# A decoder layer on one core: where the second norm's scale and shift are applied, which engines do the last norm, and how many expert rows are gathered in the first half of the u stage

## The chip, the cores and the metric

One core of one Trainium2 chip runs the whole kernel. The metric is the device time of one execution in microseconds (us). "TensorE" and PE are the same engine, as are VectorE and DVE, ScalarE and ACT, GpSimd and POOL, SyncE and SP; the profile uses the short names. Line numbers (L1053) are those of the kernel before.

## The reference, cut to what matters

One layer, 256 tokens of width 2048, everything in float32. Two attention groups, then a product-key lookup of experts, then a gated embedding, each followed by a layer norm:

```python
x = layer_norm(alpha * x + mix_out, ln_g[0], ln_b[0])
# peer_ffn: 8 heads, top 16 of 128 x 128 keys each, so 128 experts for a token
act = gelu(einsum('thed,td->the', u[eidx], x)); ffn = einsum('the,thed->td', gates * act, v[eidx])
x = layer_norm(alpha * x + ffn, ln_g[1], ln_b[1])          # the second norm
gate = sigmoid(x @ ple_gate)                               # 2048 x 2048
x = layer_norm(alpha * x + gate * (p @ ple_proj), ln_g[2], ln_b[2])   # the last norm
# layer_norm(x, g, b) = (x - mean) * rsqrt(var + eps) * g + b over the 2048 columns
```

## The kernel before

**Stages in order.** The projections and the two attentions (0 to about 350 us), the output product and the first norm, the queries and their scores (to about 530 us), then the lookup, the second norm, the gate product and the last norm. Token tiles are 128 tokens; there are two (t = 0, 1). Natural rows are tokens by partition and columns along it; transposed tiles are columns by partition.

**The lookup.** For 156 of the 256 tokens the kernel computes all 16,384 experts: the u stage has 128 blocks `ia` of 128 experts each (`u_block`, L983: load 1 MB of `peer_u`, 16 matmuls in the source, each run as two on the chip), then the v stage runs over the same blocks twice, for the two halves of the output columns (`v_block`, L1064, half a MB for each block). The other 100 tokens (`NSP`) go another way: their chosen experts' rows are gathered, 100 gathers of `u_rows` and 100 of `v_rows`, each an indirect DMA of 128 rows of 8 KB (1 MB), and VectorE multiplies and sums them (L841, L851). `sparse_work` (L808) is a generator that issues one gather for each step. `gathers(n)` (L800) adds n to a running sum and takes a step for each whole one, so the constants set gathers per block: `GQ` 1.8 for a query, `GU` 0.64 for a block of u's first half (64 blocks, L1027), `GUG` 0.75 for its second, `GVG` 0.42 and `GV` 0.35 for the blocks of v. All that is left is issued near the end of v (three blocks before the six that are held back).

A gather waits for its place: ahead of each, SP moves one element to `mark` (L871) behind the weight loads that it has queued, and GpSimd copies it (L872) before it issues the gather (L874). There are four gather buffers (`NGB`); a buffer comes free when VectorE has used it. The top-16 selection (`topk_work`, L762) runs on VectorE as a generator too, one step for each block of u's first half, and its instructions and the uses of the gathers keep their program order on VectorE. Weights (`wf`, L105) are prefetched into five buffers by SP's queue.

**Order of instructions.** The framework orders the instructions of each engine by its own timeline estimate. `keep(...)` (`tc.keep_in_program_order`) pins an instruction: pinned instructions of an engine stay in the order of the source among themselves; others may move around them.

**End of v and residual rows.** The last six blocks are held back (`STAG`) and run for j = 0 to 7 (L1158), each j one column tile of 128. Between them stand `natural_out` (L891, the gathered tokens' sums), `third_sums`, and `res2` (L1105), which transposes finished column tiles of XF back into natural rows x2[t] and takes their statistics. `stats2` (L1190) holds mean, rstd and -mean*rstd for each token tile; the power is on GpSimd (L483).

**Second norm** (`ln2`, L1200). x2[t] is normed in four chunks of 512 columns, alternately on VectorE (L1208) and ScalarE (L1206), without g and b. TensorE transposes 16 tiles of 128 x 128 for each t (L1214), four to a PSUM bank. `ln_cols` (L501) applies g and b to each transposed tile, as a scale and a shift of each partition, alternately on VectorE (L510) and ScalarE (L507), into `ln_xx`; then ScalarE rounds two tiles at a time to the matmul's format as the high part (L518) and VectorE subtracts it for the low part (L519), both into X2. `LB` is the number of tiles at a time. The natural rows get g and b separately: `natural_x2` (L1262) loads them for one chunk, spread over all partitions, and GpSimd multiplies and adds (L1269, L1270).

**Gate product.** Four chunks c of 512 output columns. For each of 16 tiles k, each token tile takes three matmuls (`mm3`, L219: high by high, high by low, low by high). The weights of a chunk are 16 parts; `Stage.split` makes the high part on ScalarE (L115) and the low part on VectorE (L116); `sg2` holds eight parts, `sg` the other eight. `gate_out` (L1226) takes the sigmoid (L1234), multiplies with the embedding (L1235), adds (L1236) and takes statistics (L1239). In the last chunk token tile 1 is cut into two halves of 256 columns.

**Last norm** (`finish`, L1242), after both token tiles: columns up to 1600 (t = 0) or 1728 (t = 1) in two passes of VectorE, L1247 ((x - mean) * g) and L1255 (* rstd + b); the rest on ScalarE and GpSimd (L1250 to L1252). Each piece is stored by a DMA of its own.

## Time and profile before

| | us |
|---|---|
| median of 3 runs (lowest, highest) | 1787.52 (1786.72, 1788.03) |
| the profiled execution | 1785.93 |
| its span | 1784.2 |
| u's first half (64 blocks of 128) | about 532 to 808 |
| v, both column halves | about 1100 to 1671 |
| first gate matmul, last gate matmul ends | 1678.95, 1772.0 |

The profile is that of one execution. Its parts: busy time of the engines; the chain of waits (what released the instruction that ended last, followed back); groups of instructions by line with their mean duration; the timeline of one engine (start, duration, engine, line, operation, output <- input, count, and in brackets how long the engine had been idle and what released it); busy time in stretches. "PEld" is TensorE's weight load, which overlaps its matmuls. Times in timelines are us from the start of the span. A matmul's duration is longer than the distance to the next one, because matmuls are pipelined.

### The profile page before, as it was taken

How to read it: one execution, taken by the hardware profiler on the slowest of the kernel's cores; microseconds unless marked ns; L12 is line 12 of the kernel's file. 1: busy time of each engine (PE TensorE's matmuls, PEld its weight loads, DVE VectorE, ACT ScalarE, POOL GpSimd, SP SyncE). 2: the span in 40 equal slices, each digit the busy share in tenths (PEclk: the TensorE clock that was granted, in tenths of full speed). 3: DMA queues.
4: the chain of work that ended last, by engine and by line, in shares of the span. 5: the costliest groups of instructions: out<-in, count | busy, mean ns of one | idle time of the engine just before them, and what ended most of it. 6: DMA issues, size and time to landing. Idle time of an engine off the chain costs nothing.

```text
span 1784.2 us, 30408 instructions
## 1 busy us (share of the span) xinstructions
PE 1755.0 (98%) x12074; PEld 1646.9 (92%) x12074; DVE 1064.5 (60%) x1706; ACT 546.5 (31%) x1363; POOL 530.9 (30%) x576
## 2 busy tenths in 40 slices
PE   8999999999999999999999999999999999999997
PEld 6888888888889999999999999999999999999786
DVE  5555589654698868455555544966433334333777
ACT  5677478733110100103333313652000000000552
POOL 0133033105346227232233332323233323220232
PEclk9999999999999999999999999999999999999999
DMA  7544644567998999999999999999999999998481
GB/s 283 191 165 166 235 143 154 195 239 253 381 418 311 421 416 416 421 421 419 420 419 410 418 419 413 404 418 399 421 421 420 421 421 420 416 411 341 167 298 65
DMA packets 99695, 606.23 MB, mean 340 GB/s; under 512 B 12824, under 2 KB 14672, under 8 KB 35648
## 3 DMA queue, kind: packets, MB, share of 16 engines
q1 hardware_dynamic: 67792, 387.91, 55.0%
q0 software_dynamic: 30320, 213.62, 29.3%
q10 hardware_dynamic: 1440, 2.75, 0.4%
q8 instruction: 95, 1.56, 0.4%
q14 instruction: 48, 0.39, 0.1%
HBM read 598.36 MB, written 6.03 MB: 339 GB/s over the span
## 4 chain that ended last, share of the span: by engine, by line
PE 89%; DMA 8%; DVE 2%; ACT 1%; issue 0%; SPq 0%; DVEq 0%; ACTq 0%
PE ps_v L1053 30%; PE ps_u L215 26%; PE ps_qk L203 7%; PE ps_q L215 6%; DMA wf<-peer_u 5%; PE ps_qk L205 3%; PE ps_v L223 2%; PE ps_v L224 2%; PE ps_v L222 2%; PE ps_gate L223 1%; PE ps_gate L222 1%; PE ps_gate L224 1%; PE ps_mix L223 1%; PE ps_mix L224 1%; PE ps_mix L222 1%; DMA wf<-peer_v 1%
## 5 line engine op out<-in xcount | busy, mean ns | idle before, releaser
L1053 PE MATMUL ps_v<-A,wf 128*128 128x156 f32 x4096 | 551.9, 297 | 0.8 <-DMA wf<-peer_v 0.8
L1053 PEld LDWEIGHTS ps_v<-A,wf 128*128 128x128 f32 x4096 | 544.5, 190 | 1.8 <-DMA wf<-peer_v 1.3
L215 PE MATMUL ps_u<-XF,wf 128*128 128x156 f32 x3904 | 531.5, 297 | 5.9 <-DMA wf<-peer_u 4.5
L215 PEld LDWEIGHTS ps_u<-XF,wf 128*128 128x128 f32 x3904 | 519.6, 190 | 10.0 <-ACT A L986 5.6
L851 DVE SCALAR_TENSOR_TENSOR y<-gb,ew,y 128x2048 f32<-128x2048 f32 x94 | 220.8, 2349 | 222.0 <-DMA gb<-v_rows,eig 221.8
L841 DVE SCALAR_TENSOR_TENSOR gb<-gb,xq 128x2048 f32<-128x2048 f32 x100 | 231.5, 2319 | 147.7 <-DMA gb<-u_rows,eig 147.7
L116 DVE TENSOR_TENSOR wl<-wf,wh 128x1024 fp32r<-128x1024 f32 (+1 forms) x199 | 213.3, 1095 | 99.0 <-ACT wh L115 97.2
L872 POOL COPY pace<-mark 1x1 f32<-1x1 f32 x200 | 116.4, 582 | 513.9 <-DMA mark<-c_iota 513.4
L115 ACT CAST wh<-wf 128x1024 fp32r<-128x1024 f32 (+1 forms) x199 | 171.8, 893 | 151.3 <-PE ps_yn L897 39.8
L203 PE MATMUL ps_qk<-X,wh 128*128 128x512 f32 x512 | 185.2, 401 | 0.0
L986 ACT ACTIVATE A<-ps_u 128x156 f32<-128x156 f32 x128 | 38.4, 300 | 442.9 <-PE ps_u L215 357.0
L874 POOL DMA_INDIRECT gb<-u_rows,eig x100 | 114.7, 1147 | 143.7 <-DVE gb L841 74.7
L874 POOL DMA_INDIRECT gb<-v_rows,eig x100 | 123.4, 1234 | 78.4 <-DVE y L851 39.0
L205 PE MATMUL ps_qk<-X,wl 128*128 128x256 f32 x512 | 145.7, 285 | 0.0
L939 ACT ACTIVATE hi<-eq,ghf 128x64 f16<-128x64 f16 x312 | 104.5, 335 | 40.6 <-DVE eq L933 35.9
L203 PEld LDWEIGHTS ps_qk<-X,wh 128*128 128x128 f32 x512 | 96.4, 188 | 21.9 <-issue 1.0
L215 PE MATMUL ps_q<-XF,wf 128*128 128x256 f32 x512 | 113.6, 379 | 0.6 <-DVE XF L510 0.6
L1114 ACT COPY x<-ps_y 128x256 f32<-128x256 f32 (+3 forms) x12 | 5.2, 439 | 350.0 <-DVE st L1113 349.8
L215 PEld LDWEIGHTS ps_q<-XF,wf 128*128 128x128 f32 x512 | 95.9, 190 | 13.1 <-DVE XF L510 0.8
L940 ACT ACTIVATE lo<-eq,glf 128x64 f16<-128x64 f16 x312 | 104.1, 334 | 0.0
L205 PEld LDWEIGHTS ps_qk<-X,wl 128*128 128x128 f32 x512 | 96.3, 188 | 2.5 <-issue 1.3
L957 DVE SCALAR_TENSOR_TENSOR A<-ps_G,A 128x30 f32<-128x30 f32 (+2 forms) x96 | 32.6, 368 | 38.0 <-PE ps_G L947 21.9
(261 smaller groups left out, 1836.1 us busy)
## 6 DMA issues: line engine op xcount, KB each, us to landing
wf<-peer_v SPq DMA_DIRECT2D x128, 1024.0 KB
wf<-peer_u SPq DMA_DIRECT2D x122, 1024.0 KB
wf<-w_qk SPq DMA_DIRECT2D x64, 512.0 KB
wf<-w_out SPq DMA_DIRECT2D x32, 512.0 KB
wf<-peer_wq SPq DMA_DIRECT2D x16, 1024.0 KB
wf<-ple_gate SPq DMA_DIRECT2D x16, 1024.0 KB
wf<-w_v SPq DMA_DIRECT2D x31, 512.0 KB
early<-peer_u SPq DMA_DIRECT2D x6, 1024.0 KB
```

What stands on the lines that cost most here:

```text
L115: self.order(nc.scalar.copy(wh, src))
L116: self.order(nc.vector.tensor_tensor(wl, src, wh.bitcast(F32), op=ALU.subtract))
L203: nc.tensor.matmul(ps, wh[:, j * P:(j + 1) * P], xt[:, dt, :], start=dt == 0, stop=False)
L205: nc.tensor.matmul(ps[:, :T], wl[:, j * P:(j + 1) * P], xt[:, dt, :T], start=False, stop=dt == ND - 1)
L215: nc.tensor.matmul(ps[:, :T - t0], wf[:, dt * P:(dt + 1) * P], xt[:, dt, t0:], start=dt == 0, stop=dt == ND - 1)
L841: keep(nc.vector.scalar_tensor_tensor(g, g, 1.0, xq[i], op0=ALU.mult, op1=ALU.mult, accum_out=eact[i][:, j:j + 1]))
L851: keep(nc.vector.scalar_tensor_tensor(ys[i], g, ew[i][:, j:j + 1], ys[i], op0=ALU.mult, op1=ALU.add))
L872: keep(nc.gpsimd.tensor_copy(pace, mark))
L874: keep(nc.gpsimd.indirect_dma_start(out=g, out_offset=None, in_=a[kind], in_offset=bass.IndirectOffsetOnAxis(ap=eig[i][:, 0, j:j + 1], axi ...
L939: nc.scalar.mul(hi[:, j, :], eq[:, j, :], ghf[:, t])
L940: nc.scalar.mul(lo[:, j, :], eq[:, j, :], glf[:, t])
L1053: return nc.tensor.matmul(ps[:, (j % 2) * NDT:(j % 2 + 1) * NDT], vf[:, j * P:(j + 1) * P], W_of(ia), start=False, stop=ia == NIA - 1 and ...
```

## The change

It has four parts.

1. `GU` goes from 0.64 to 0.60. `GUG`, `GVG` and `GV` stay.
2. The second norm's g and b rows are loaded earlier, by SP, one chunk at a time into XF as its column tiles come free (`rows2`, pinned). For five of the eight pieces (token tile by chunk) VectorE applies norm, g and b to the natural rows in two passes ahead of the transposes: (x - mean) * g, then * rstd + b. For the other three (chunk 1 of t = 0, chunks 2 and 3 of t = 1) ScalarE norms them, applies g and b to the transposed tiles, and VectorE multiplies and adds g and b on the natural rows later. GpSimd does none of it.
3. For those five pieces the high and low parts come straight from the PSUM bank of the transposes, up to four tiles at a time (`ln2_hi`, `ln2_lo`). Everything from there to the end of the first gate chunk is pinned in an order written out by hand: transposes, parts, splits of the weights and gate matmuls of single k. The gate matmuls of the last chunk are pinned too, and in chunk 2 all splits for chunk 3 come ahead of token tile 1's `gate_out`.
4. The last norm is on VectorE alone. Token tile 0's statistics and first pass stand ahead of token tile 1's first half, its second pass ahead of the second half; the pieces are of 512 columns for t = 0 and 640, 640, 512, 256 for t = 1.

```diff
-GU, GUG = 0.64, 0.75
+GU, GUG = 0.60, 0.75
-LB = 2
+    gb2 = [XF[:, 4 * c:4 * c + 4, :].rearrange("p (i d) n -> p i (d n)", i=2) for c in range(NCH)]
+    def rows2(c):
+        for i, src in enumerate(("ln_g", "ln_b")):
+            keep(nc.sync.dma_start(
+                gb2[c][:, i], a[src][1:2, c * 512:(c + 1) * 512].to_broadcast([P, 512])))
...
         elif j == 6:
+            rows2(0)
...
         elif j == 7:
+            rows2(1)
...
+    rows2(2)
     res2(0, 12, 2)
...
+    def ln2_pass(i, t, c0, n):
+        mv, rstd, nmr = stats2[t]
+        s = slice(c0, c0 + n)
+        row = gb2[c0 // 512][:, i, c0 % 512:c0 % 512 + n]
+        if i == 0:
+            keep(nc.vector.scalar_tensor_tensor(x2[t][:, s], x2[t][:, s], mv[:, 0:1], row,
+                                                op0=ALU.subtract, op1=ALU.mult))
+        else:
+            keep(nc.vector.scalar_tensor_tensor(x2[t][:, s], x2[t][:, s], rstd, row,
+                                                op0=ALU.mult, op1=ALU.add))
+    def ln2_T(t, d0, nd):
+        ps = pbank(pp, "ps_x2T")
+        for j in range(nd):
+            keep(nc.tensor.transpose(ps[:, j * P:(j + 1) * P],
+                                     x2[t][:, (d0 + j) * P:(d0 + j + 1) * P], ident))
+        return ps[:, :nd * P].rearrange("p (j n) -> p j n", j=nd)
+    def ln2_hi(t, d0, src):
+        nd = src.shape[1]
+        keep(nc.scalar.copy(X2[:, d0:d0 + nd, t * P:(t + 1) * P], src))
+    def ln2_lo(t, d0, src):
+        nd = src.shape[1]
+        hi = X2[:, d0:d0 + nd, t * P:(t + 1) * P]
+        keep(nc.vector.tensor_tensor(X2[:, d0:d0 + nd, T + t * P:T + (t + 1) * P], src,
+                                     hi.bitcast(F32), op=ALU.subtract))
+    def act_norm(t, c):
...
+    def act_cols(d0, ps):
...
+    def natural_gb(t, c):
...
-    ln2(0)
-    ln2(1, range(ND // 8))
+    gw = [sg.load(a["ple_gate"][0, i]) for i in range(2, 4)]
+    rows2(3)
+    pss = [pbank(pa, "ps_gate") for _ in range(NT)]
+    act_norm(0, 1)
+    for i in range(2):
+        ln2_pass(i, 0, 0, 256)
+    ps = ln2_T(0, 0, 2)
+    ln2_hi(0, 0, ps)
+    ps1 = ln2_T(0, 4, 4)
+    for i in range(2):
+        ln2_pass(i, 0, 256, 256)
+    ps2 = ln2_T(0, 2, 2)
+    ln2_hi(0, 2, ps2)
+    ln2_lo(0, 0, ps)
+    gate_k(0, 0, 1)
+    ln2_lo(0, 2, ps2)
+    gate_k(0, 1, 3)
+    xx = act_cols(4, ps1)
+    ln2_hi(0, 4, xx)
+    ln2_pass(0, 1, 0, 512)
+    ln2_lo(0, 4, xx)
+    ln2_pass(1, 1, 0, 512)
+    both(1, 1)
+    gate_k(0, 3, 5)
+    ps = ln2_T(1, 0, 4)
+    ln2_hi(1, 0, ps)
+    gate_k(0, 5, 6)
+    ln2_lo(1, 0, ps)
+    act_norm(1, 2)
+    act_norm(1, 3)
+    more_parts(2)
+    gate_k(0, 6, 8)
+    gate_k(1, 0, 1)
+    ps = ln2_T(1, 4, 4)
+    ln2_hi(1, 4, ps)
+    ln2_lo(1, 4, ps)
+    gate_k(1, 1, 2)
+    both(0, 2)
...
+    gate_k(1, 6, 8)
+    gate_k(0, 8, 10)
+    ps = ln2_T(0, 12, 4)
+    ln2_hi(0, 12, ps)
+    ln2_lo(0, 12, ps)
+    more_parts(2)
+    gate_k(0, 10, 12)
+    for d0, k0, k1 in ((8, 12, 14), (12, 14, 16)):
+        ps = ln2_T(1, d0, 4)
+        xx = act_cols(d0, ps)
+        natural_gb(1, d0 // 4)
+        ln2_hi(1, d0, xx)
+        ln2_lo(1, d0, xx)
+        gate_k(0, k0, k1)
+    natural_gb(0, 1)
+    parts1 = list(sg2.parts(a["ple_gate"][1, 0]))
+    gate_k(1, 8, 16)
     for c in range(NCH):
         if c == NCH - 1:
+            pass2(0, [512, 1024, 1536], *mr)
             gate_out(c, 1, ps_half, 256, 256)
             break
...
-        natural_x2(c + 1, nc.sync)
...
+        gate_mm(pss[0], 0, parts, 0, 512, keep)
+        gate_mm(pss[1][:, :256], 1, parts, 0, 256, keep)
+        gate_mm(pss[2][:, :256], 1, parts, 256, 256, keep)
         gate_out(c + 1, 0, pss[0], 0, 512)
+        mr = finish_stats(0)
+        pass1(0, [512, 1024, 1536], *mr)
         gate_out(c + 1, 1, pss[1][:, :256], 0, 256)
         ps_half = pss[2][:, :256]
-    for t in range(NT):
-        finish(t, gr3, br3)
+    mr = finish_stats(1)
+    pass1(1, [640, 1280, 1792], *mr)
+    pass2(1, [640, 1280, 1792], *mr)
```

`act_norm(t, c)` norms 512 columns in place on ScalarE; `act_cols` applies g and b to four transposed tiles from PSUM, one activate for each; `natural_gb` is a multiplication and an addition of 512 columns on VectorE. `gate_k(t, k0, k1)` is `mm3` for single k, pinned; `both(t, c)` is the two passes over 512 columns; `more_parts(n)` splits n parts of the second half of chunk 0's weights; `finish_stats`, `pass1` and `pass2` are the parts of the former `finish`, without its share for ScalarE and GpSimd.

More of the change, by code (lines that the diff above doesn't have):

```diff
@@ new lines, in act_norm @@
+    def act_norm(t, c):
+        s = slice(c * 512, (c + 1) * 512)
+        mv, rstd, nmr = stats2[t]
+        keep(nc.scalar.activation(x2[t][:, s], x2[t][:, s], AF.Identity, bias=nmr, scale=rstd))
+    def act_cols(d0, ps):
+        xx = l2.tile([P, 4, P], F32, name="ln_xx", tag="ln_xx", bufs=2)
+        for j in range(4):
+            keep(nc.scalar.activation(xx[:, j], ps[:, j], AF.Identity,
+                                      bias=bT[:, 1, d0 + j:d0 + j + 1],
+                                      scale=gT[:, 1, d0 + j:d0 + j + 1]))
+        return xx
@@ L1273, in build, with finish_stats @@
-    sg.order = sg2.order = keep
-    parts = [parts0, gate_parts(0, 1)]
-    ln2(1, range(ND // 8, ND // 4))
+            keep(nc.vector.bn_stats(st3[t][:, 2 * c + j // 256, :],
+                                    x2[t][:, c * 512 + j:c * 512 + j + 256]))
+    def finish_stats(t):
+        mv = l2.tile([P, 2], F32, name="mv3", tag="ln_mv", bufs=2)
+        keep(nc.vector.bn_aggr(mv, st3[t]))
+        rstd = l2.tile([P, 1], F32, name="rstd3", tag="ln_rstd", bufs=2)
+        keep(nc.vector.tensor_scalar_add(rstd, mv[:, 1:2], LN_EPS))
+        nc.gpsimd.tensor_tensor(rstd, rstd, half_neg, op=ALU.pow)
+        return mv, rstd
@@ L1276, in build @@
+    ps = ln2_T(1, 0, 4)
[12 more added lines that the diff above has]
+    both(0, 2)
+    more_parts(1)
     for t in range(NT):
         keep(nc.scalar.copy(em3[:, t], pse[t]))
[L1278 to L1283 removed]
+    gate_k(1, 2, 6)
```

110 lines of the change are left out of this document (41 added, 69 removed).

## The prediction

> **What bounds the kernel now.** I read the page's engine table first, then busy time by stretches, then the timelines of the two places that the diff touches.
>
> ```profile
> PE 1755.0 (98%) x12074; PEld 1646.9 (92%) x12074; DVE 1064.5 (60%) x1706; ACT 546.5 (31%) x1363; POOL 530.9 (30%) x576
> 721.00:815.00 94.00, 89.99 (x668) 87.54 (x668) 45.45 (x51) 15.80 (x53) 28.84 (x31) 1.00 1.01 421
> 1240.00:1400.00 160.00, 160.00 (x1209) 160.00 (x1209) 65.87 (x31) 0.00 (x0) 50.40 (x55) 1.00 1.01 418
> 1600.00:1672.00 72.00, 72.00 (x538) 70.41 (x537) 31.46 (x48) 10.90 (x22) 3.50 (x4) 1.00 0.76 290
> 1672.00:1785.00 113.00, 96.29 (x475) 78.99 (x473) 87.31 (x152) 54.83 (x113) 36.28 (x32) 0.96 0.49 181
> ```
>
> A row of the stretches reads: stretch, its length, busy us and instructions of PE, PE's weight loads, DVE, ACT and POOL, TensorE clock, DMA share, GB/s. TensorE sets the time: it is idle only in u's first half (4.0 us in the second row) and in the last stretch (16.7 us). The clock is full. DMA moves 418 to 421 GB/s for as long as gathers run, so 1 MB (1,048,576 bytes) costs 2.49 us; after 1600 us it has room (share 0.76). So an edit is worth what it takes from those two idle places; elsewhere it must only not break TensorE's stream.
>
> **The change, part 1: fewer gathers in u's first half (GU 0.64 to 0.60).** TensorE's own timeline there:
>
> ```profile
> 648.54 72.33 PE ps_u L215 x544
> 734.19 4.48 PE L215 MATMUL ps_u<-XF,wf 128*128 128x156 f32 x32 [0.47 <-ACT A L986]
> 739.16 4.48 PE L215 MATMUL ps_u<-XF,wf 128*128 128x156 f32 x32 [0.49 <-DMA wf<-peer_u]
> ...
> 768.96 30.25 PE L215 MATMUL ps_u<-XF,wf 128*128 128x156 f32 x224 [0.48 <-ACT A L986]
> 799.70 4.48 PE L215 MATMUL ps_u<-XF,wf 128*128 128x156 f32 x32 [0.49 <-DMA wf<-peer_u]
> ```
>
> The first row (the chain of waits) gives a block of 32 matmuls undisturbed: 72.33 x 32 / 544 = 4.25 us. From 734.19 to 768.96 seven blocks take 34.77 us instead of 29.8: about 4.6 us lost once the three pairs of gate transposes between them are taken off, each block waiting for its `wf`. The stall at 799.70 adds 0.7. Why there? The gathers:
>
> ```profile
> 700.00:720.00 20.00, 5.28 (x6) 1.00 1.02 423
> 720.00:740.00 20.00, 3.83 (x4) 1.00 1.01 419
> 741.11 0.18 POOL L872 COPY pace<-mark 1x1 f32<-1x1 f32 x1 [1.37 <-DMA mark<-c_iota]
> ```
>
> (The first two rows are L874 alone: gathers issued per 20 us.) While DVE selects the top keys, gathers fall behind; then they catch up, 10 in the 40 us from 700. In those 40 us TensorE wants 40 / 4.25 = 9.4 MB of `peer_u` and the gathers bring 10 MB: 19.4 x 2.49 = 48.3 us of DMA in 40. The prefetched buffers cover some, TensorE waits for the rest. At 741 POOL waits for a mark again: the backlog is gone.
>
> With 0.60, 64 x 0.04 = 2.56 fewer gathers fall into this half. About 1.6 of them (40 blocks) lie ahead of the burst: 1.6 x 2.49 = 4.0 us of DMA time less, against 5.3 us lost. The steady need falls from 1.64 MB per 4.25 us (4.08 us of DMA, 96%) to 1.60 (3.98, 94%), so the stall at 799 should go too. Bounds: nothing (the burst is set by DVE's order, not by the marks) and 5.3. I take **4.0**, nearest to the DMA time that is removed.
>
> The 2.56 gathers land at the end of v's second half. Each needs 1 / 0.35 = 2.9 blocks of 2.1 us there, so the last gather comes about 15 us later than this row:
>
> ```profile
> 1613.77 0.96 POOL L874 DMA_INDIRECT gb<-v_rows,eig x1 [0.16 <-DVE gb L849]
> 1651.61 0.68 DVE L900 TENSOR_TENSOR x<-x,ps_yn 96x512 f32<-96x512 f32 x1 [24.36 <-PE ps_yn L897]
> ```
>
> The sums that need them start at 1651; the splits ahead of them (L115, L116 on `y`) move from 1607 to about 1622, the last use from 1625 to about 1640. That is the cover; its price if it were gone would be one us for each us past 1650. DMA has 0.24 x 72 = 17 us free there against 6.4 added. Cost: nothing.
>
> **Part 2: second norm and the start of the gate product.**
>
> ```profile
> 1672.33 2.74 PE L1124 MATMUL ps_emb<-wp,pf 128*128 128x512 f32 x6
> 1675.22 2.03 PE L1214 MATMUL ps_x2T<-ident,x 128*128 128x128 f32 x16 [0.15 <-DVE x L1208]
> 1678.95 0.50 PE L222 MATMUL ps_gate<-wh,X 128*128 128x512 f32 x1 [1.70 <-ACT X L518]
> 1688.20 0.50 PE L222 MATMUL ps_gate<-wh,X 128*128 128x512 f32 x1 [1.69 <-ACT X L518]
> 1704.62 1.01 DVE wl L116
> 1705.67 0.51 PE ps_gate L223
> 1674.53 1.95 DVE L1208 TENSOR_SCALAR x<-x,ln_mv,ln_rstd 128x512 f32<-128x512 f32 x4 [0.57 <-POOL ln_rstd L483]
> ```
>
> TensorE is done with the embedding at 1675.07 and has the first gate matmul at 1678.95. Gaps: 1.70, 1.69 and, by the chain's two rows, about 0.5 at 1705 for `wl`.
>
> The new first chain, from rstd ready (1674.53): the first pass over 256 columns needs only the mean and runs before; the second takes 0.42 (L1236's 256-column form below): 1674.95. Two transposes after 1675.07 (2.03 for 16, 0.27 of it latency) end at 1675.5. ACT does the norm of chunk 1 first (0.80), so the copy of `hi` (0.41) runs 1675.65 to 1676.06; eight more transposes keep TensorE till 1676.4: the first gate matmul comes 2.5 us earlier. From there every wait is one of a handful, and I walked them in the pinned order with these rows:
>
> ```profile
> L116 DVE TENSOR_TENSOR wl<-wf,wh 128x512 fp32r<-128x512 f32 x56 | 35.2, 697 | 0.1
> L519 DVE TENSOR_TENSOR X<-ln_xx,X 128x256 fp32r<-128x256 f32 x16 | 9.5, 612 | 0.3 <-ACT X L518 0.3
> L510 DVE TENSOR_SCALAR ln_xx<-ps_x2T,gT,bT 128x128 f32<-128x128 f32 x16 | 6.1, 404 | 2.7 <-ACT ln_xx L507 2.6
> L1236 DVE SCALAR_TENSOR_TENSOR x<-x,sig 128x256 f32<-128x256 f32 x2 | 0.8, 419 | 0.0
> L1247 DVE SCALAR_TENSOR_TENSOR x<-x,ln_mv,g_row 128x512 f32<-128x512 f32 x4 | 2.8, 744 | 0.0
> L507 ACT ACTIVATE ln_xx<-ps_x2T,bT,gT 128x128 f32<-128x128 f32 x16 | 6.9, 456 | 3.9 <-DVE ln_xx L510 3.7
> L518 ACT CAST X<-ln_xx 128x256 fp32r<-128x256 f32 x16 | 6.1, 407 | 0.3
> L1277 ACT COPY XF<-ps_emb 128x512 f32<-128x512 f32 x2 | 1.1, 584 | 0.0
> L1270 POOL TENSOR_TENSOR x<-x,XF 128x512 f32<-128x512 f32 x8 | 13.2, 1673 | 0.0
> L1269 POOL TENSOR_TENSOR x<-x,XF 128x512 f32<-128x512 f32 x8 | 10.3, 1308 | 44.6 <-DMA XF<-ln_g 44.6
> ```
>
> DVE loses L1208 (2.0), L510 (6.1) and L519 (9.5): 17.6 us. It gains five chunks with g and b in two passes (10 x 0.7), three chunks where they follow on natural rows (6 x 0.65) and eight subtractions of 512 columns (8 x 0.7, by L116; from PSUM the L900 row above has 0.68): 16.5. POOL loses all of L1269 and L1270 (23.5 us). ACT has 3 norms, 12 activates of 128 columns, 9 copies: 12.5 us for 16.0. So no engine has more work, and ACT and DVE no longer hand each 128-column piece of one bank to each other (2.6 and 3.7 us of waits in the L510 and L507 rows). In my walk the pinned TensorE stream waits 0.25 us (`lo` of tiles 4 to 7), 0.4 (rows of token tile 1) and some 0.6 in restarts; the `lo` pieces later arrive 0.3 to 0.9 us ahead, and `wl` of chunk 1 is made early, so the 0.5 goes. Gaps of 3.9 and the 1.3 us from 1675.07 to 1676.4, mostly filled now, become about 1.8: **3.4** earlier at the end of chunk 0. Later chunks are TensorE-bound before and after. Bounds: 5.2 (all idle time of this stretch) and a loss (rival 3).
>
> The rows of g and b come by SP now. Chunk 0's wait for transposes of about 1665 and are wanted at 1674; the slowest row for such a load is 5.9 us, and DMA is at 0.18 of its share between:
>
> ```profile
> XF<-ln_g POOLq DMA_DIRECT2D x1, 256.0 KB, 5.9
> 1667.00:1670.00 3.00, 3.00 (x26) 3.00 (x25) 2.11 (x6) 1.17 (x3) 0.00 (x0) 1.00 0.18 76
> ```
>
> Queued behind these waits on SP are only `ple_gate` loads that are split after 1683; cost nothing, price a us per us if they landed after 1674.
>
> **Part 3: the last norm.**
>
> ```profile
> 1760.00:1772.00 12.00, 11.97 (x92) 11.32 (x90) 8.56 (x14) 2.04 (x4) 3.70 (x3) 1.00 0.07 24
> 1772.00 0.38 ACT L1234 ACTIVATE sig<-ps_gate 128x256 f32<-128x256 f32 x1 [3.63 <-PE ps_gate L224]
> 1768.47 3.98 DVE L1255 SCALAR_TENSOR_TENSOR x<-x,ln_rstd,b_row 128x512 f32<-128x512 f32 x3
> 1773.16 0.41 DVE L1235 TENSOR_TENSOR sig<-sig,XF 128x256 f32<-128x256 f32 x1
> 1775.06 2.27 DVE L1247 SCALAR_TENSOR_TENSOR x<-x,ln_mv,g_row 128x512 f32<-128x512 f32 x3
> 1777.24 3.47 DVE L1255 SCALAR_TENSOR_TENSOR x<-x,ln_rstd,b_row 128x512 f32<-128x512 f32 x3
> ```
>
> TensorE ends at 1772.0, the span at 1784.2: a tail of 12.2. The last sigmoid is ready at 1772.38, but DVE takes it at 1773.16, busy with token tile 0. With the order pinned, tile 0's 512 columns come first and its passes lie under the last 96 matmuls, of 256 columns each; the first row has 92 such, a few wider, in 12 us, more than the 9.4 us of DVE work in them (2.1 and 1.3 for two outputs, 0.5, 5.5 for two passes). So the sigmoid is taken 0.05 after it is ready: 0.7 gained. The step to the first pass stays 1.90. Both passes now cover 2048 columns instead of 1728: by L1247, 2.27 for 1728, so 2.75 each. The second pass lost time to POOL (3.47 for 1728) and is now 2.75: the two together are 5.5 against 5.65. The last DMA carries 128 KB instead of 352. It now takes 3.5 us from DVE's last end (1780.71) to the span's end; between 3.5 and half of it I take 3.2. New tail: 0.4 + 0.05 + 1.9 + 5.5 + 3.2 = 11.05, **1.2** less. Bounds: 2 less, 0.5 more.
>
> The Trainium skill (DMA: Bandwidth & Descriptors, Anatomy of one DMA) gives a DMA 2.0 us and its bytes at 436 GB/s: as an estimate, 2.3 us for 128 KB against 2.8 for 352. By it the landing would be 3.0 and the whole sum 0.2 us lower.
>
> **Sum**, against the profiled execution (1785.93, span 1784.2, so 1.7 around it): 4.0 + 3.4 + 1.2 = 8.6 us; span 1775.6, execution 1777.3. The runs shown lie 1.6 above that execution (median 1787.52), so I name **1778.9** as their median.
>
> **Rivals.**
> 1. Fewer gathers give nothing (17%). If DMA alone set the pace from 580 us to the last gather, moving bytes inside that stretch would change nothing. For: 418 to 421 GB/s in all of it. Against: TensorE is busy 160.00 of 160.00 us there, and the loss sits in one burst. Left 4.6: 1782.9. The Trainium skill (DMA: Bandwidth & Descriptors, Specifications) puts HBM at about 358 GB/s for a core; a need of 1.64 MB per 4.25 us is 405, and by that rule this rival holds. The trace moves 421, so I give the rule little.
> 2. The pinned order gains nothing ahead of chunk 1 (11%): waits of 0.4 us at each of eight hand-overs eat the 3.4. Left 5.2: 1782.3.
> 3. Slower (11%). In the pinned order every group runs transposes, copy of `hi`, subtraction of `lo`, gate matmuls, and TensorE cannot go round a late one. One bare chain costs 0.27 + 0.58 + 0.68 plus hand-overs, 1.7 us. If DVE, with some 21 us of work (16.5 and eight splits) in the 24 us of chunk 0, runs late, the eight chains lie open: 13.6 us instead of the 1.8 above, 8.6 - 11.8 = 3.2 lost, and 7.2 if part 1 gives nothing too: 1790.7 to 1794.7. It decides from five chains open (8.6 / 1.7).
> 4. The parts cancel to within 0.2% (10%): 1785 to 1788, half of part 1 and two or three chains open.
>
> **How the numbers follow.** The forecast (1775.5 to 1781.5) has 51%. A measurement of this kernel tells about 0.2% (3.6 us) from no change. Faster by more: forecast, most of rivals 1 and 2, 76%; same 13%; slower 11%. The range takes the larger bounds (5.3 + 5.2 + 2 would be 1775.0) at its low end and rivals 1, 2 and half of 4 at its high end: 1775.5 to 1786.0.
>
> **What would show it.** Part 1: no blocks of 4.97 us from 734 to 769, the half ending 4 us sooner, the last gather near 1624 to 1629. Part 2: first gate matmul 1.9 us after rstd is ready (4.4 now), no idle of TensorE over 0.5 before chunk 1. Part 3: DVE idle before the last sigmoid, second pass about 2.75, tail 11. I am wrong if the burst stays, if TensorE waits for `hi` or `lo` again and again, or if the g and b rows land after 1674.

## The result and the profile after

The changed kernel takes 1777.25 us, the median of five runs (1776.11 to 1778.52); the kernel before took 1786.72 beside it (1784.2 to 1788.03). The ratio is 0.9948, with a 95% interval of 0.9933 to 0.9962: 7 to 12 us less. The forecast was 1778.9. The profiled execution took 1776.11, its span is 1774.2, against 1785.93 and 1784.2 before. The 10.0 us between the spans lie in three places:

| Event (us from the start of the span) | before | after | gained up to here | gained since the row above |
|---|---|---|---|---|
| first matmul of u's second half (`ps_G`) | 808.68 | 804.59 | 4.1 | 4.1 |
| first sum of the gathered tokens (`ps_yn`) | 1650.38 | 1644.51 | 5.9 | 1.8 |
| power of the second norm starts (POOL) | 1673.92 | 1668.04 | 5.9 | 0.0 |
| last gate matmul ends | 1771.97 | 1762.88 | 9.1 | 3.2 |
| span ends | 1784.2 | 1774.2 | 10.0 | 0.9 |

So part 1 is the first three rows (5.9), part 2 the fourth (3.2), part 3 the last (0.9).

Busy time by engine, and the stretches that answer to those of before (length, then busy us and instructions of PE, PE's loads, DVE, ACT and POOL, clock, DMA share, GB/s), in the changed kernel:

```profile
PE 1752.7 (99%) x12074; PEld 1647.6 (93%) x12074; DVE 1058.7 (60%) x1699; ACT 540.3 (30%) x1347; POOL 516.4 (29%) x554
```

```profile
721.00:815.00 94.00, 93.01 (x713) 92.23 (x712) 44.01 (x50) 16.15 (x55) 27.26 (x28) 1.00 1.01 420
1600.00:1672.00 72.00, 70.27 (x505) 66.26 (x504) 38.07 (x64) 14.41 (x32) 9.90 (x13) 1.00 0.85 325
1672.00:1775.00 103.00, 90.61 (x453) 75.78 (x451) 76.66 (x131) 45.43 (x88) 3.67 (x5) 0.95 0.45 168
```

TensorE's idle time from 721 to 815, the end of u's first half, fell from 4.0 us to 1.0. But the second row, where it had none, now has 1.7, and it is new. TensorE's timeline in the changed kernel, with the idle time before each group and what ended it:

```profile
739.32 4.48 PE L214 MATMUL ps_u<-XF,wf 128*128 128x156 f32 x32 [0.50 <-DMA wf<-peer_u]
744.29 8.72 PE L214 MATMUL ps_u<-XF,wf 128*128 128x156 f32 x64 [0.49 <-DMA wf<-peer_u]
...
762.11 42.64 PE L214 MATMUL ps_u<-XF,wf 128*128 128x156 f32 x320
...
1580.15 62.70 PE L1043 MATMUL ps_v<-A,wf 128*128 128x156 f32 x472
1643.98 0.80 PE L1043 MATMUL ps_v<-A,wf 128*128 128x156 f32 x4 [1.13 <-DMA wf<-peer_v]
...
1669.28 0.41 PE L1216 MATMUL ps_x2T<-ident,x 128*128 128x128 f32 x2
1670.23 0.87 PE L1216 MATMUL ps_x2T<-ident,x 128*128 128x128 f32 x6 [0.54 <-ACT x L1234]
1670.86 0.48 PE L221 MATMUL ps_gate<-wh,X 128*128 128x512 f32 x1
...
1675.11 0.63 PE L1216 MATMUL ps_x2T<-ident,x 128*128 128x128 f32 x4 [0.26 <-DVE x L1210]
```

The reader is to see three things. Two waits for `wf` are left of the burst, and then ten blocks run without a stop. At the end of v stands a wait of 1.13 us that the kernel before didn't have. And the second norm gives TensorE its first gate matmul 2.8 us after the power starts (5.0 before), with no wait of more than 0.54.

The 1.8 us between the first and the second row of the table were waits, too, which the prediction had not looked for. All waits for loads from 815 us on in TensorE's timeline of the kernel before:

```profile
840.88 4.51 PE L215 MATMUL ps_u<-XF,wf 128*128 128x156 f32 x32 [0.54 <-DMA wf<-peer_u]
845.86 4.51 PE L215 MATMUL ps_u<-XF,wf 128*128 128x156 f32 x32 [0.41 <-DMA wf<-peer_u]
850.83 13.39 PE L215 MATMUL ps_u<-XF,wf 128*128 128x156 f32 x96 [0.17 <-DMA wf<-peer_u]
...
1543.92 4.51 PE L1053 MATMUL ps_v<-A,wf 128*128 128x156 f32 x32 [0.19 <-DMA wf<-peer_v]
1549.08 2.39 PE L1053 MATMUL ps_v<-A,wf 128*128 128x156 f32 x16 [0.65 <-DMA wf<-peer_v]
```

They make 1.96 us, and each costs another 0.24, since a block behind a wait takes 4.48 us where an undisturbed one takes 4.25: 3.2 in all. None of them is left in the changed kernel; after 744 its only wait for such a load is the one at 1643.98, which costs 1.4. The difference is the 1.8.

The tail, on DVE, in the changed kernel:

```profile
1763.33 0.43 DVE L1265 TENSOR_TENSOR sig<-sig,XF 128x256 f32<-128x256 f32 x1 [1.72 <-ACT sig L1264]
...
1765.19 2.73 DVE L1285 SCALAR_TENSOR_TENSOR x<-x,mv,g_row 128x640 f32<-128x640 f32 x4
1767.84 2.73 DVE L1290 SCALAR_TENSOR_TENSOR x<-x,rstd,b_row 128x640 f32<-128x640 f32 x4
```

DVE is done at 1770.57, and the span ends 3.63 us later; below this is called the landing. The stretches behind DVE's end (the last two figures are DMA share and GB/s):

```profile
1770.60:1772.60 2.00, 0.00 (x0) 0.00 (x0) 0.00 (x0) 0.00 (x0) 0.00 (x0) 0.50 0.91 325
1772.60:1774.16 1.56, 0.00 (x0) 0.00 (x0) 0.00 (x0) 0.00 (x0) 0.00 (x0) 0.50 0.00 0
```

Output moves for 2.0 us more. In the 1.56 us after that no DMA moves anything.

### The profile page after: what moved, and what is told of

Read it like the earlier page. It is cut to its first block, busy times and chain, and to the rows that moved or that the text cites. A ratio compares the mean times of both kernels' runs of the same rounds, so it can differ in the third digit from the quotient of the medians.

```text
span 1774.2 us, 30337 instructions
## 1 busy us (share of the span) xinstructions
PE 1752.7 (99%) x12074; PEld 1647.6 (93%) x12074; DVE 1058.7 (60%) x1699; ACT 540.3 (30%) x1347; POOL 516.4 (29%) x554
## 3 DMA queue, kind: packets, MB, share of 16 engines
q8 instruction: 95, 1.56, 0.4%
## 4 chain that ended last, share of the span: by engine, by line
PE 93%; DMA 4%; DVE 1%; ACT 0%; issue 0%; SPq 0%; POOL 0%; DVEq 0%; ACTq 0%
PE ps_v L1043 30%; PE ps_u L214 29%; PE ps_qk L202 7%; PE ps_q L214 6%; PE ps_qk L204 4%; DMA wf<-peer_u 2%; PE ps_v L222 2%; PE ps_v L223 2%; PE ps_gate L221 2%; PE ps_gate L223 2%; PE ps_gate L222 2%; PE ps_v L221 2%; DMA wf<-peer_v 1%; PE ps_mix L222 1%; PE ps_mix L223 1%; PE ps_mix L221 1%
## 5 line engine op out<-in xcount | busy, mean ns | idle before, releaser
L862 POOL COPY pace<-mark 1x1 f32<-1x1 f32 x200 | 108.2, 541 | 514.6 <-DMA mark<-c_iota 514.2
L864 POOL DMA_INDIRECT gb<-v_rows,eig x100 | 137.2, 1372 | 90.1 <-DVE y L841 54.7
L864 POOL DMA_INDIRECT gb<-u_rows,eig x100 | 122.1, 1221 | 126.3 <-DVE gb L831 67.2
```

The source lines that it names most:

```text
L862: keep(nc.gpsimd.tensor_copy(pace, mark))
L864: keep(nc.gpsimd.indirect_dma_start(out=g, out_offset=None, in_=a[kind], in_offset=bass.IndirectOffsetOnAxis(ap=eig[i][:, 0, j:j + 1], axi ...
```

## The experiments

Each kernel was timed in five rounds beside the kernel before. A ratio is to the kernel before, with its 95% interval; 0.001 is 1.8 us. In the expectations, theory A says that part 1 is worth the 5.9 us of the table; B that it is worth the 4.0 of u's first half; C that it is worth nothing, since DMA sets the pace.

### Which part is worth what

**gu_alone**, the kernel before with part 1 alone:

```diff
-GU, GUG = 0.64, 0.75
+GU, GUG = 0.60, 0.75
```

> The kernel before with GU 0.60 and nothing else. Theory A (the gathers taken out ahead of DVE's top-key burst remove the DMA debt of u's first half, and with it the waits for wf that this debt left in u's second half and in v): by the two profiles 5.9 us, 1780.8. Theory B (part 1 is worth only what u's first half lost, 4.0 us, and the other 1.9 us that v gained belong to something else in the change): 1782.7. Theory C (DMA alone sets the pace up to the last gather, so bytes moved within that stretch give nothing, and the norms made the whole gain): 1786.7.

Measured: 1780.68 us, ratio 0.9975 (0.9965 to 0.9986): 4.5 us less (2.5 to 6.2). In its profile the first `ps_yn` stands at 1644.64, 5.7 us earlier than before. C is out. The intervals of the times don't part A from B; the profile says A.

**gu_back**, the changed kernel with that line set back:

```diff
-GU, GUG = 0.60, 0.75
+GU, GUG = 0.64, 0.75
```

> The changed kernel with GU back at 0.64; both norms as changed. Theory A: 5.9 us lost again, 1783.2, with blocks of 4.98 us back at 734 to 769 and stalls for wf at about 841 to 851 and 1549. Theory B: 1781.3. Theory C: 1777.3. If the parts add, its gain over the kernel before is 4.1 us (3.2 for the second norm and 0.9 for the last): 1782.6.

Measured: 1781.67, ratio 0.9980 (0.9971 to 0.9989): 3.6 us less than before (2.0 to 5.2) for the two norms, where the table has 4.1. The median lies nearer to B's 1781.3 than to A's 1783.2, but the interval holds both. Together with gu_alone that is 8.1 us, where the ratio of the whole change makes 9.3; the parts add within their intervals. TensorE's timeline of gu_back shows all the waits come back:

```profile
732.18 4.48 PE L214 MATMUL ps_u<-XF,wf 128*128 128x156 f32 x32 [0.48 <-DMA wf<-peer_u]
...
757.06 4.48 PE L214 MATMUL ps_u<-XF,wf 128*128 128x156 f32 x32 [0.31 <-DMA wf<-peer_u]
...
836.49 4.48 PE L214 MATMUL ps_u<-XF,wf 128*128 128x156 f32 x32 [0.37 <-DMA wf<-peer_u]
...
1548.63 2.39 PE L1043 MATMUL ps_v<-A,wf 128*128 128x156 f32 x16 [0.17 <-DMA wf<-peer_v]
```

And the wait at the end of v is gone: its `ps_yn` at 1649.93 has no wait before it. From the power to the last gate matmul it takes 94.84 us, to the hundredth what the changed kernel takes, so parts 1 and 2 don't touch each other.

**norm3_old**, the changed kernel with `finish` as before, both token tiles after the loop (the last chunk's matmuls and sums aren't pinned in it either, so it sets back all of that at once):

```diff
-    mr = finish_stats(1)
-    pass1(1, [640, 1280, 1792], *mr)
-    pass2(1, [640, 1280, 1792], *mr)
+    for t in range(NT):
+        finish(t, gr3, br3)
```

> The changed kernel with the last norm as before: both token tiles after the loop, their last 448 and 320 columns on ACT and POOL, the last chunk's matmuls and sums not pinned. Theory A (the last norm's change is worth what the tail shrank, 0.9 us, since TensorE ends at the same time either way): 1778.2, tail 12.2 us after the last matmul. Rival: pinning the last chunk costs TensorE something that the tail hides (part 3 is worth nothing): 1777.3. Rival: tile 0's passes under the matmuls free more than the tail shows, 2 us: 1779.3.

Measured: 1778.14, ratio 0.9958 (0.9944 to 0.9971). By the medians part 3 is worth 0.9 us, by the profile too: the tail after the last gate matmul is 12.2 us there and 11.3 in the changed kernel. The intervals overlap, so the 0.9 rests on the profiles.

### Where part 1's gain comes from

The prediction put the loss into one burst at 734 to 769 and the gain into the 1.6 gathers ahead of it (A1 below). The other reading is A2: DMA is full from 580 us to the last gather, so a wait that goes at one place comes back at the next, unless gathers leave that stretch.

**lean_first**, the kernel before with as many gathers in u's first half, but 1.6 of them after the burst instead of before it:

```diff
-        gathers(GU)
+        gathers(0.60 if ia < 40 else 0.7067)
```

> The kernel before with u's first half at 0.60 gathers a block for its first 40 blocks and 0.7067 for the other 24: as many in all as at 0.64 (40.96), 1.6 of them later. Theory A1 (the loss sits in the burst at 734 to 769 alone, and 1.6 gathers less ahead of it are the gain, as the prediction had it): the seven blocks of 4.97 us go, 4.0 us faster, 1781.7. Theory A2 (DMA is full from 580 us to the last gather; a wait that goes at one place comes back at the next where the prefetched buffers run out, unless gathers leave the stretch for the end of v): the waits move to u's second half (840 to 860) and v, and the time stays within 1 us of the kernel before, 1784.7 to 1786.7.

Measured: 1785.43, ratio 0.9998 (0.9989 to 1.0007). TensorE's timeline of lean_first:

```profile
735.10 4.48 PE L215 MATMUL ps_u<-XF,wf 128*128 128x156 f32 x32 [0.22 <-DMA wf<-peer_u]
...
839.30 4.51 PE L215 MATMUL ps_u<-XF,wf 128*128 128x156 f32 x32 [1.38 <-DMA wf<-peer_u]
...
854.20 8.91 PE L215 MATMUL ps_u<-XF,wf 128*128 128x156 f32 x64 [0.34 <-DMA wf<-peer_u]
```

The burst is shorter (four waits from 735 to 750, for six from 739 to 764), and what went there is back a hundred us later, with 1.38 us at one place. TensorE comes to that load 2.4 us earlier than in the kernel before (837.92 for 840.34) and loses the lead at this load and the next ones. A1 expected 4.0 us and got none. It falls.

**lean_last**, the mirror of it:

```diff
-        gathers(GU)
+        gathers(0.68 if ia < 40 else 0.5733)
```

> The kernel before with 0.68 gathers a block for the first 40 blocks of u's first half and 0.5733 for the other 24 (40.96 in all, 1.6 of them earlier). Theory A1: the burst is 1.6 gathers worse, 4.0 us slower, 1789.7. Theory A2: more waits before 769, fewer after, the time within 1 us, 1784.7 to 1786.7.

Measured: 1789.47, ratio 1.0019 (1.0010 to 1.0028), 3.4 us slower. That looks like A1. The stretch from 760 to 815 tells why it isn't; first the kernel before, then lean_last:

```profile
760.00:815.00 55.00, 53.47 (x404) 52.37 (x403) 28.58 (x33) 9.54 (x38) 19.31 (x18) 1.00 1.01 420
```

```profile
760.00:815.00 55.00, 55.00 (x418) 55.00 (x418) 26.15 (x30) 6.97 (x26) 13.62 (x15) 1.00 0.99 399
```

In lean_last's row DMA has too little to do: 399 GB/s for 420, so 55 x 21 / 420 = 2.8 us of DMA time are lost. The hole is at 770 to 790: weight loads are issued only as fast as TensorE frees their buffers (one each 4.2 to 4.5 us), and no gather is issued from 759.30 to 776.91, where GpSimd waits for a gather buffer:

```profile
776.91 2.77 POOL L874 DMA_INDIRECT gb<-u_rows,eig  x1 [8.40 <-DVE gb L841]
```

A2 as I had written it (within 1 us) missed this. With it the reading is sharper: in this stretch DMA time that is not used is not had again, and the kernel got longer by about as much (3.4 for 2.8).

**gug_71**, the kernel before with the 2.56 gathers taken out of u's second half:

```diff
-GU, GUG = 0.64, 0.75
+GU, GUG = 0.64, 0.71
```

> The kernel before with the 2.56 gathers taken out of u's second half (0.71 a block for 0.75) instead of its first. Theory A1 (the burst at 734 to 769 alone costs): the burst stays, nothing gained, 1786. Theory A2 (DMA full from 580 us to the last gather): the waits at 734 to 769 stay, those at 840 to 854 and at 1543 to 1549 go (about 2.8 us with their restarts), and the last peer_v comes 1.1 us late: 1.7 us faster, 1784.3.

Measured: 1784.05, ratio 0.9985 (0.9977 to 0.9994), 2.7 us less (1.1 to 4.1). TensorE's timeline of gug_71, with all waits for loads after 758:

```profile
758.25 4.48 PE L215 MATMUL ps_u<-XF,wf 128*128 128x156 f32 x32 [0.32 <-DMA wf<-peer_u]
846.67 4.48 PE L215 MATMUL ps_u<-XF,wf 128*128 128x156 f32 x32 [0.50 <-DMA wf<-peer_u]
1649.37 0.80 PE L1053 MATMUL ps_v<-A,wf 128*128 128x156 f32 x4 [1.28 <-DMA wf<-peer_v]
```

The burst stays whole (seven waits up to 758), one wait is left of those at 840 to 855, both in v are gone, and the end of v has a wait of 1.28. It doesn't matter that the gathers left behind the burst; what counts is that they left the full stretch. The profile shows less than the times: this execution's `ps_yn` is 0.5 us earlier than before, as its u's first half, the same as before, ended 1.4 us later (810.10); from there to `ps_yn` it gains 1.9.

So part 1 gains because its 2.56 gathers (6.4 us of DMA time by the prediction's 2.49 us for 1 MB) go to a place where DMA had room. Before and after, in this order, the end of v:

```profile
1630.00:1645.00 15.00, 15.00 (x115) 15.00 (x115) 0.00 (x0) 0.00 (x0) 0.00 (x0) 1.00 0.77 276
```

```profile
1630.00:1645.00 15.00, 13.87 (x103) 13.56 (x103) 3.20 (x2) 0.00 (x0) 0.00 (x0) 1.00 0.90 338
```

The second row has the price, 1.13 us of TensorE (1.4 with the restart).

### What the late gathers cost

**gate_late**, the changed kernel with the last `peer_v` loads ahead of the gate's first weights in SP's queue:

```diff
     for ia in range(NIA - STAG, NIA):
         held.append(v_load(1, ia))
-        if ia in (NIA - STAG + 1, NIA - 1):
-            gw.append(sg2.load(a["ple_gate"][0, len(gw)]))
+    for i in range(2):
+        gw.append(sg2.load(a["ple_gate"][0, i]))
```

> The changed kernel with the two first loads of the gate's weights issued behind the last three loads of peer_v instead of between them. Theory (the 1.13 us that TensorE waits at 1643.98 for the last peer_v is the price of the 2.56 late gathers: that load is issued 5.3 us ahead of its use and now shares DMA with more): issued one block pair sooner, at about 1633, it is there in time, 1.1 us faster, 1776.1; the gate's weights land just before their buffers for splits come free at 1645. Rival (DMA is the limit there too, and something else is late instead): 1777.3 or more.

Measured: 1775.06 (1773.92 to 1776.94), ratio 0.9939 (0.9925 to 0.9952). In the changed kernel the last of these loads is on the chain of waits:

```profile
1637.58 6.36 DMA wf<-peer_v
```

TensorE had work up to 1642.85 (the row of 472 matmuls), 5.3 us after that issue. In gate_late the load is issued one place sooner, at 1633.63, and v, now 476 matmuls in one row, runs into `ps_yn` without a stop:

```profile
1580.44 63.24 PE L1043 MATMUL ps_v<-A,wf 128*128 128x156 f32 x476
1643.40 0.50 PE L887 MATMUL ps_yn<-wh,sel 128*96 128x512 f32 x1
```

`ps_yn` comes 1.1 us earlier, as expected, and the power too (1666.91 for 1668.04). This is the fastest version that was run. Against the changed kernel the medians differ by 2.2 us and the ratios by 0.0009; the intervals overlap, so more than the 1.1 us of the profile is not shown.

**late_58** and **late_56**: gate_late with still fewer gathers in u's first half. The diff is that of late_58; late_56 has 0.56 in its place.

```diff
-GU, GUG = 0.60, 0.75
+GU, GUG = 0.58, 0.75
```

> gate_late with GU 0.58: 1.28 gathers more leave u's first half for the end of v, 3.2 us of DMA time. Theory A2: the waits that are left up to 760 us (4 to 6 of them, some 3 us with their restarts) halve, nothing new is late: 1773.5. Rival (the last gathers are now too close to their use at 1643, and the end of v gives it back): 1775 to 1776.

> gate_late with GU 0.56: 2.56 gathers more leave u's first half, 6.4 us of DMA time. Theory A2: at most 3 us are left to gain in u's first half; the last gather comes at about 1635, its sums at 1648, and what is issued at the end of v shares DMA with it: between 1772 and 1777, with waits at 1640 to 1660. Rival (late gathers cost nothing, as the prediction said): 1772.3.

Measured: late_58 1777.73, ratio 0.9952 (0.9939 to 0.9964); late_56 1788.24, ratio 1.0019 (1.0008 to 1.0030). Both expectations were too good. In late_58 v is 1.2 us ahead of gate_late when its first finished tile is transposed (1534.16 for 1535.38), most of what was expected. Then the wait for the last load is back, 0.92 us and a restart, and at `ps_yn` (1643.35 for 1643.40) nothing remains. In late_56 the end of v gives back more than everything. TensorE's timeline of late_56:

```profile
1646.78 1.41 PE L1043 MATMUL ps_v<-A,wf 128*128 128x156 f32 x4 [3.14 <-DMA wf<-peer_v]
...
1660.36 3.62 PE L898 MATMUL ps_y<-sel,gb 128*128 128x32 f32 x16 [4.45 <-DVE gb L841]
```

The first wait stands where DMA is full again (420 GB/s from 1643.6 to 1646.8). For the second, the last gather is issued at 1630.21. The last two products on DVE come behind sums that wait for `ps_yn`, at 1651.51 and here:

```profile
1657.97 2.33 DVE L841 SCALAR_TENSOR_TENSOR gb<-gb,ew 128x2048 f32<-128x2048 f32 x1
```

It ends at 1660.30, and `third_sums` (L898) waits for it. And the waits cost more than themselves. The clock that TensorE was granted around the second one is the figure in front of the last two:

```profile
1656.00:1660.00 4.00, 0.00 (x0) 0.00 (x0) 4.00 (x7) 0.00 (x0) 0.00 (x0) 1.00 0.00 0
1660.00:1664.00 4.00, 3.64 (x17) 3.64 (x18) 2.71 (x5) 0.00 (x0) 0.00 (x0) 0.51 0.08 16
1664.00:1668.00 4.00, 4.00 (x23) 4.00 (x22) 2.54 (x5) 2.44 (x5) 0.00 (x0) 0.63 0.63 246
```

From `ps_yn` to the power it takes 32.4 us there, 23.5 in the changed kernel. So from 0.64 to 0.60 there is a gain, from 0.60 to 0.58 none, and at 0.56 it is lost.

### What in the second norm gains: the order or the pieces

**norm2_free**, the changed kernel with the new passes and parts in the framework's own order (the planner's), the weight splits still pinned:

```diff
-            keep(nc.vector.scalar_tensor_tensor(x2[t][:, s], x2[t][:, s], mv[:, 0:1], row,
-                                                op0=ALU.subtract, op1=ALU.mult))
+            (nc.vector.scalar_tensor_tensor(x2[t][:, s], x2[t][:, s], mv[:, 0:1], row,
+                                                op0=ALU.subtract, op1=ALU.mult))
...
-            mm3(pss[t], X2, k, t, *parts0[k], k == 0, k == ND - 1, keep)
+            mm3(pss[t], X2, k, t, *parts0[k], k == 0, k == ND - 1)
```

(and so in `ln2_T`, `ln2_hi`, `ln2_lo`, `act_norm`, `act_cols` and `natural_gb`)

> The changed kernel with the order of the second norm and of chunk 0's gate product left to the planner (passes, transposes, hi, lo, gate matmuls not pinned; the weight splits stay pinned). Theory A (the gain of 3.2 us there is the natural rows and parts from PSUM; the written order only secures it): within 1 us of the changed kernel, 1777.3 to 1778.3. Rival (the order is what gains; the planner puts transposes of the second token tile ahead of the first gate matmuls, whose rows come later): the 3.2 us go, 1780.5 or more, with TensorE idle over 1 us before chunk 1.

Measured: 1780.53, ratio 0.9968 (0.9956 to 0.9980): 3.3 us above the changed kernel by the medians. The rival holds. From the power to the last gate matmul it takes 97.66 us, 2.8 more than the changed kernel and as long as gu_alone (97.67), which has the old norm. TensorE's timeline of norm2_free:

```profile
1674.53 1.69 PE L1216 MATMUL ps_x2T<-ident,x 128*128 128x128 f32 x12 [2.15 <-DVE x L1210]
...
1677.59 0.66 PE L1216 MATMUL ps_x2T<-ident,x 128*128 128x128 f32 x4 [0.67 <-ACT ln_xx L1240]
```

The planner puts twelve transposes ahead of the first gate matmul, and they wait for DVE's passes.

**order_only**, the written order with the old pieces in it: norm without g and b, g and b by columns after the transposes, parts from SBUF, the natural rows' g and b on POOL. It takes up to four tiles at a time through these steps, where the kernel before took two (`LB`), so it is not the old norm reordered and nothing else.

```diff
-            keep(nc.vector.scalar_tensor_tensor(x2[t][:, s], x2[t][:, s], mv[:, 0:1], row,
-                                                op0=ALU.subtract, op1=ALU.mult))
+            keep(nc.vector.tensor_scalar(x2[t][:, s], x2[t][:, s], mv[:, 0:1], rstd,
+                                         op0=ALU.subtract, op1=ALU.mult))
...
+                if j % 2:
+                    keep(nc.scalar.activation(xx[:, j], src[:, j], AF.Identity, bias=b, scale=g))
+                else:
+                    keep(nc.vector.tensor_scalar(xx[:, j], src[:, j], g, b, op0=ALU.mult,
+                                                 op1=ALU.add))
...
-        keep(nc.vector.tensor_tensor(x2[t][:, s], x2[t][:, s], gb2[c][:, 0], op=ALU.mult))
+        nc.gpsimd.tensor_tensor(x2[t][:, s], x2[t][:, s], gb2[c][:, 0], op=ALU.mult)
```

> The changed kernel with its written order of the second norm and of chunk 0, but the pieces of before in it: norm with mean and rstd only, g and b by columns of 128 after the transposes, ACT and DVE in turn, parts from SBUF, g and b of the natural rows on POOL. Theory A3 (the written order alone makes the 3.2 us, since the new pieces in the planner's order made none of it): from rstd to the last gate matmul about 95 to 96 us, 1777.3 to 1778.3. Rival (order and pieces are both needed: the old pieces make each chain of columns, hi and lo longer by a hand-over and 0.8 us, and the pinned TensorE waits for each): 97 us or more, 1779.5 to 1783.

Measured: 1793.20, ratio 1.0041 (1.0027 to 1.0055), 16 us above the changed kernel and slower than the one before. Both theories expected far less. TensorE's timeline of order_only:

```profile
1687.03 0.80 PE L221 MATMUL ps_gate<-wh,X 128*128 128x512 f32 x1 [3.98 <-ACT X L1230]
...
1704.57 0.79 PE L221 MATMUL ps_gate<-wh,X 128*128 128x512 f32 x1 [1.67 <-ACT X L1230]
```

Behind the first gate matmul stand eight waits of 0.50 to 3.98 us (the two longest above); they make 10.8, and the clock falls behind the two longest. The stage takes 112.9 us. Where the wait of 3.98 comes from is seen on DVE and POOL; their timelines of order_only:

```profile
1681.19 3.38 DVE L115 TENSOR_TENSOR wl<-wf,wh 128x512 fp32r<-128x512 f32 x2 [1.22 <-ACT wh L114]
1684.50 0.40 DVE L1227 TENSOR_SCALAR ln_xx<-ps_x2T,gT,bT 128x128 f32<-128x128 f32 x1
```

```profile
1681.05 1.30 POOL L1247 TENSOR_TENSOR x<-x,XF 128x512 f32<-128x512 f32 x1 [1.62 <-PE ps_x2T L1213]
1682.43 1.59 POOL L1248 TENSOR_TENSOR x<-x,XF 128x512 f32<-128x512 f32 x1
```

A split that takes 0.70 alone takes 1.69 beside POOL's multiplications, and the columns that TensorE needs stand behind it in DVE's pinned order: about 2 us for the two splits. The rest of the wait is the chain behind them, from 1684.50 to 1687.03: four columns handed to and fro between DVE and ACT, then the copy. So the four cases of the stage are: old pieces and planner's order 97.7 to 98.5, new pieces and planner's order 97.7, old pieces (four tiles at a time) and written order 112.9, both new 94.8. As they were built here, neither half of part 2 gains alone.

### The landing

**tail_inter**, the changed kernel with the two passes of token tile 1 interleaved:

```diff
-    pass1(1, [640, 1280, 1792], *mr)
-    pass2(1, [640, 1280, 1792], *mr)
+    for f, i in ((pass1, 0), (pass1, 1), (pass2, 0), (pass1, 2), (pass2, 1), (pass1, 3),
+                 (pass2, 2), (pass2, 3)):
+        f(1, [640, 1280, 1792], *mr, slice(i, i + 1))
```

> The changed kernel with the last norm's two passes of token tile 1 interleaved by piece, so that the first output pieces leave 0.9 to 1.7 us sooner; the same eight instructions. Theory (the landing of 3.6 us is the backlog of 1 MB of output that DVE makes in 2.7 us): it falls to about 3.0, 1776.6. Rival (the landing is a fixed time of the last DMA, whatever its size and what lies ahead of it): 3.6 as before, 1777.3.

Measured: 1777.37, ratio 0.9953 (0.9939 to 0.9966), no different from the changed kernel. DVE's last row in tail_inter:

```profile
1769.68 1.14 DVE L1290 SCALAR_TENSOR_TENSOR x<-x,rstd,b_row 128x512 f32<-128x512 f32 x2
```

DVE ends at 1770.82, the span at 1774.2: a landing of 3.38 us for 3.63, of which the 0.6 that I expected is less than half. The first pieces left sooner, and it hardly helped. Backlog is the smaller part of the landing: behind DVE's end output moves for another 1.8 us here and 2.0 in the changed kernel. Then come 1.6 us in both (1.5 in the kernel before) without any DMA traffic, in which the trace has only semaphore and drain instructions of the program's end.

## Why the prediction was right, and where not

**The time.** The sum was 8.6 us off the profiled execution, and the profiles make it 9.8; the median of 1777.25 lies 1.65 us under the forecast. By parts: 5.9 for 4.0, 3.2 for 3.4, 0.9 for 1.2. That the sum came so near is in part luck: in part 1 it missed a gain of 3.2 us and a price of 1.4, which have opposite signs.

**Part 1** is the step that failed, as working more than as a number. "About 1.6 of them (40 blocks) lie ahead of the burst: 1.6 x 2.49 = 4.0" made a local account: gathers ahead of the burst count, the others don't. lean_first moved just these 1.6 and gained nothing; gug_71 moved 2.56 others and gained 2.7 us with the burst untouched. What counts is that gathers leave the stretch in which DMA is full. The gain is then what TensorE has to lose behind that place: 4.1 us in u's first half and 3.2 in waits after it, 7.3 ahead of the price. The 6.4 us of DMA time (2.56 x 2.49) are near that but are not its measure: gug_71 took out the same 6.4 where only 3.2 us of waits lay behind, and with the 1.5 of its wait at the end put back its gain is 4.2 us (2.6 to 5.6). The account had ruled out the place where the 3.2 lay: "it is idle only in u's first half (4.0 us in the second row) and in the last stretch". I had not read TensorE's rows from 815 to 1600, where the same debt made five more waits. All this is good to about a microsecond, by which u's first half differs between executions that are the same up to its end: 804.59 in the changed kernel and 805.47 in gate_late, 808.68 before and 810.10 in gug_71.

"The 2.56 gathers land at the end of v's second half ... Cost: nothing" was wrong by the wait of 1.13 us, 1.4 with its restart. The cover was counted as free DMA time over 72 us and as time to the gathers' own use, and both were there: the last gather moved from 36.6 us ahead of `ps_yn` to 23.4 (15 were forecast, 13.2 measured; it is issued at 1621.12, where 1624 to 1629 was named). What was not asked is which other transfer stands beside them. It was the last `peer_v`, issued 5.3 us ahead of its use. In the kernel before it was in time with 5.0 (issued at 1644.85, used at 1649.83); now it moves beside more traffic. 7.3 less 1.4 is the 5.9 of the table.

**Rival 1** had the mechanism (DMA is full from 580 to the last gather) and drew the wrong end from it. Moving bytes inside that stretch gains nothing (lean_first; lean_last even loses 3.4 us); these bytes left it.

**Part 2** was sized rightly. The first gate matmul comes 2.2 us sooner after the power (2.5 forecast); the waits are 0.54 (ACT's norm of chunk 1, L1234, which six transposes wait for), 0.26 (rows of token tile 1; 0.4 forecast) and restarts, and chunk 1's wait for `wl` is gone. The bar "no idle of TensorE over 0.5" was missed by 0.04. The rows of g and b were issued on SP from 1659.07 on and nobody waited for them.

**Rivals 2 and 3** did not come true here, since the pieces are short enough. order_only shows that rival 3 was real: with the old pieces in the pinned stream TensorE waits eight times, 10.8 us in all, where the prediction had priced eight open chains at 13.6. What the prediction lacked is the clock behind the longest waits: half of it for 3.4 and 6.8 us is another 5. The loss is 15 us (112.9 for 97.7).

**Part 3.** DVE takes the last sigmoid 0.04 us after it is ready (0.05 forecast), 1.86 to the first pass (1.90), 5.38 for the two (5.5). The mis-sized term is the landing: 3.2 forecast, 3.63 measured. I had let all of it shrink with the last piece, from 352 KB to 128, and it did not: 3.49, 3.63 and 3.38 us in the kernel before, the changed one and tail_inter. In each of the three, 1.5 to 1.6 us come after the last byte of output has moved, whatever the size of the last piece. The estimate by the Trainium skill (DMA: Bandwidth & Descriptors, Anatomy of one DMA), 2.0 us and the bytes at 436 GB/s, is fitted to DMAs that GpSimd issues; these stores are issued on SP. It would make 3.0 of the landing, and these three landings don't agree with it.

**Not settled:** what in those 1.5 to 1.6 us could be shortened; and the times of late_58, whose profiled execution (1775.29) is its fastest and whose median lies 2.4 above that.

## What to carry to other kernels

Where one engine and DMA are both full for long, as here, don't price a transfer by the wait next to it: a wait that goes at one place can come back at the next. Bytes that leave the full stretch gain, and no more than the waits that lie behind the place they leave; ask then which load stands just in time at the place they go to, and issue it sooner. A written order and the pieces that it needs can be one change: in a pinned stream each open chain is paid in full, and the order that gained 3 us with short chains lost 15 with long ones.

## What the runs showed of the hardware

**The clock falls by stretches of 3.41 us, so a wait's place counts beside its length.** In norm2_free TensorE waited 2.27 us at the end of v, and half the clock followed (clock, DMA share and GB/s are the last three):

```profile
1645.57 0.80 PE L1043 MATMUL ps_v<-A,wf 128*128 128x156 f32 x4 [2.27 <-DMA wf<-peer_v]
1642.95:1646.36 3.41, 1.14 (x8) 0.91 (x7) 0.00 (x0) 0.00 (x0) 0.00 (x0) 1.00 0.84 300
1646.36:1649.78 3.42, 3.42 (x11) 2.29 (x10) 2.40 (x5) 2.35 (x4) 0.00 (x0) 0.50 0.06 24
1649.78:1653.19 3.41, 3.41 (x21) 2.87 (x21) 3.41 (x8) 0.13 (x1) 0.00 (x0) 1.00 0.10 38
```

(The first row is TensorE's timeline, the others are stretches.) Half the clock for 3.41 us is 1.7 lost, so this wait cost about 4; from `ps_yn` to the power it takes 25.1 us there and 23.5 in the changed kernel. In late_56 and order_only half the clock lasts 3.41 or 6.83 us, and the full clock between is a multiple of 3.41 as well (10.24, 13.65). Counted in steps of 3.41 from such changes (in the kernel before, from where its full clock starts, at 7.70), the stretches in which TensorE stood longest while the clock was full, and some shorter ones:

| Run | stretch starts | TensorE idle in it, us | clock after it |
|---|---|---|---|
| order_only | 1683.27 | 3.4 | 0.50 |
| late_56 | 1656.71 | 3.4 | 0.50 |
| late_56 | 1643.05 | 2.8 | 0.50 |
| norm2_free | 1642.95 | 2.3 | 0.50 |
| before | 1676.82 | 1.7 | 1.00 |
| order_only | 1700.33 | 1.6 | 0.50 |
| norm2_free | 1670.26 | 1.3 | 1.00 |

The wait of 2.15 at 1674 in norm2_free is the last row: it falls on two stretches and left the clock full. So 2.3 us of idle time in one stretch was enough, and 1.3 was not. Between them these runs don't settle it, since 1.6 was followed by a drop and 1.7 was not. The Trainium skill (TensorE: Matmul & The Clock Gate, Why this matters for your kernels) advises against idle gaps of more than about 3 us. These runs show drops behind shorter ones, so the margin is smaller than that.

**DVE beside POOL.** In order_only a 512-column split on DVE took 1.69 us beside POOL's multiplication and addition, and 0.70 without them.
